# A list scheduler's model of TensorE: new durations, new latencies and a price for changing the shape of the product

## The chip, the cores and the metric

The kernel runs on one core of a Trainium2 chip. The metric is the device time of one execution in microseconds (us), taken as the median of several runs. Beside the runs there is one profiled execution, from which the trace comes; it has a time of its own.

A core has engines that work side by side, each through its own list of instructions and in the order of that list: PE (TensorE, matrix products and transposes), DVE (VectorE), ACT (ScalarE), POOL (GpSimd) and SP (SyncE, which here only sends DMA transfers). They wait for one another by semaphores.

## The reference

A trunk of two layers on x of shape (1, 256, 1024), all in float32. Each layer:

```python
h = rms_norm(x, attn_norm[l])
proj = h @ w_in[l]
r_q, r_k, r_v, r_g, n_q, n_kv, n_g, gm_z = jnp.split(proj, split_points, axis=-1)
ret_o = retention(rope(r_q), rope(r_k), r_v, r_g)          # 6 heads, chunks of 128
nsa_o = nsa(n_q, n_kv, n_g, ...)                           # 6 heads: compressed | selected | window, gated
gm_o  = spatial_gating(gm_z, gm_ws[l], gm_b[l])            # 4 heads of a causal gMLP
x = x + concatenate([ret_o, nsa_o, gm_o]) @ w_out[l]
h = rms_norm(x, ffn_norm[l])
gate, up = jnp.split(h @ w_gate_up[l], 2, axis=-1)         # d_ff = 2816
x = x + (silu(gate) * up) @ w_down[l]
```

Within `nsa`, queries and keys are normalised head by head, blocks of 32 keys and values are compressed to one token each by a small MLP (`cmp_w1`, gelu, `cmp_w2`), and three softmax outputs are mixed by sigmoid gates.

## The kernel before

Everything lies in SBUF for both row tiles of 128 positions; only the weights stream from memory. Each weight piece arrives in one of three buffers `wst`; ACT casts it to a rounded format (`whi`, fp32r, a "cast" below), DVE subtracts to get the rest (`wlo`, a "split" below), and PE multiplies in three terms: activations high with `whi`, high with `wlo`, low with `whi`. These products, 512 columns wide in most places (384 and 274 in some), are called main products here. They write to the four accumulators `acc`; all else of PE (transposes, scores, small products) goes through four banks `sm`. The activations are `hcat`, with a high and a low half.

A layer projects in seven parts: `nk` (keys), `nq` (queries), `gm` (gMLP), `nv` (values of the compression and the gates), `rq`, `rk`, `rg` (retention), each with 48 main products. What follows from a part runs beside the main products of the next ones. The steps that are spoken of below:

- `nk_tile` (keys): ACT squares, DVE sums (`nkr_ss`), ACT and DVE take the inverse root (`nkr_z`, `nkr_y`), DVE scales to `w1k`, PE transposes (`sm<-cst,w1k`), ACT and DVE write `Kh` and `Kl`. `nq_tile` does the same for the queries by `nqr_*`, `w2k` and `Q`, with three transposes for each row tile.
- `compress`: transposed tokens are copied by DVE to `aT`, PE multiplies them with `w` in 64 small products, and a gelu by single steps on DVE follows.
- `unit`: scores `sm<-Kh,Q` on PE, bias and row maximum on DVE (the custom instruction that writes `S`, a "mask step" below, printed as ISA in an order), exp on ACT, scaling by `asm` on DVE, transposes. `pv` multiplies with the values; its first product is `sm<-pcT,vbd`.
- `setup_bias`: POOL sends a small table to memory (`scr`) and reads it back as the bias `B`.

The order of the instructions isn't written by hand. The code of each step is a generator ("thread") that hands over operations; the class `Desk` (from L257) plays through the kernel with a model of time while it is built, and gives each engine its list in the order in which the model starts the operations. The model has a duration for each operation (`_cost_PE` from L199, and one for each other engine), a latency from an operation's end to its reader (`LAT`), and a price for a change of ACT's table. In `run` the engine that can start first is taken, and of its ready operations the one with the least `rank`: priority of the thread, then the time at which it became ready. A main product has the priority 1000, so any step that is ready goes before it; main products fill the rest. The model decides the order alone: on the chip every operation takes what it takes, and PE waits wherever its list names a product whose data isn't there.

All operations are issued by the one line L196, so the rows of the trace are told apart by the names of their tiles.

Of the kernel before, what the change touches and what calls it, by code (L numbers as in the profile page):

```python
# [166 lines left out]
class Op:  # L167
    def __init__(self, engine, call, dur, table, lat, prio, banks):
        self.engine, self.call, self.dur, self.table = engine, call, dur, table
        self.lat, self.prio, self.banks = lat, prio, banks  # L170


def _free(ap):
    n = 1
    for s in ap.shape[1:]:
        n *= s
    return n


def _psum(*aps):  # L180
    return any(getattr(a, "space", None) == bass.MemoryType.PSUM for a in aps)


class Engine:


# [3 lines left out]
    def __getattr__(self, method):  # L190
        fn = getattr(self.eng, method)

        def make(*a, prio=None, lat=True, **k):
            dur, table = getattr(self, "_cost_" + self.name)(method, a, k)
            banks = {x.tensor.name for x in (*a, *k.values()) if _psum(x)}
            return Op(self.name, lambda: fn(*a, **k), dur, table, lat, prio, banks)  # L196

        return make

    def _cost_PE(self, method, a, k):  # L200
        if method == "transpose":
            return 108, None
        n = _free(a[0])
        load = 0.42 * _free(a[1])
        if a[2].dtype == F32R:
            return max(0.422 * n, load + 27), None
        if a[0].shape[0] == 64 and a[0].base_partition() == 64:
            return 54 if n > 64 else 27, None
        return 2 * max(0.844 * n, 2 * load), None

    def _cost_DVE(self, method, a, k):
# [45 lines left out]


class Desk:
    LAT = {"PE": 170, "DVE": 150, "ACT": 190, "POOL": 200, "DMA": 2000, "SWDMA": 4500}  # L260
    TABLE = 1300
    COLD = 5500.0

    def __init__(self, preload):
        self.preload = preload
        self.free = {e: 0.0 for e in self.LAT}
        self.free["DMA"] = 1500.0
        self.pending = {e: [] for e in self.LAT}
        self.table = None
        self.cur = None  # L270
        self.live = 0
        self.after = 0
        self.banks = {}
        self.given = 100
# [74 lines left out]
    def run(self, gen):  # L349
        th = Thread(gen, 1000, 0.0)  # L350
        self.live = 1
        self._step(th, None)
        while self.live:
            best = None
            for e, reqs in self.pending.items():
                if reqs:
                    s = max(self.free[e], min(self._ready(r) for r in reqs))
                    if best is None or s < best[0]:
                        best = (s, e)
            assert best is not None, "every thread waits"  # L360
            now, e = best
            reqs = self.pending[e]

            def rank(r):
                th, ops = r
                p = ops[0].prio
                p = th.prio if p is None else p() if callable(p) else p
                if ops[0].table is not None and ops[0].table != self.table and now - th.t < 4000:
                    p += 500
                return (p, th.t, th.n)  # L370

            r = min((r for r in reqs if self._ready(r) <= now), key=rank)
            reqs.remove(r)
            th, ops = r
            t = now
            for op in ops:
                if op.table is not None and op.table != self.table:
                    t += self.TABLE
                    self.table = op.table
                    self.preload(op.table)  # L380
                op.call()
                t += op.dur * (2 if e == "PE" and t < self.COLD else 1)
            self.free[e] = t
            for op in ops:
                for b in op.banks:
                    self.banks.setdefault(b, {})[e] = t + self.LAT[e]
            th.t = t + (self.LAT[e] if ops[-1].lat else 0)
            self._step(th, None)


class Trunk:
# [71 lines left out]
    def stream_load(self):  # L463
        for i in range(L * len(PIECES)):
# [8 lines left out]
            self.st[i] = st  # L473
            self.desk.fire(self.loaded[i], self.desk.LAT["DMA"])
            if i < len(self.ev_w):
# [70 lines left out]
    def warm_up(self):  # L546
# [5 lines left out]
        while not self.started:  # L552
            n = 256 if self.desk.free["PE"] < Desk.COLD else 128
            yield self.PE.matmul(ps[:, :n], w[:, :128], w[:, :n], start=True, stop=True, lat=False, prio=2000)
# [3 lines left out]
    def load_start(self):  # L558

        SP, fire, lat = self.SP, self.desk.fire, self.desk.LAT["DMA"]  # L560
        yield SP.dma_start(self.ident, self.d["cst"][:, C_ID : C_ID + 128], lat=False)
# [1054 lines left out]
```

## Time and profile before

| | us |
|---|---|
| median of 3 runs | 646.93 (646.89 to 647.25) |
| profiled execution, its own time | 646.46 |
| span of the trace in it | 644.7 |
| mean granted clock of TensorE, share of full | 0.997 |
| PE busy | 635.1 |
| DVE busy | 452.9 |
| ACT busy | 364.8 |

A row of the timeline gives the start in us, the time that it takes, engine, line, operation, what it writes and reads, shapes, and with xN how many neighbouring instructions of that kind it holds together; in square brackets stands how long the engine was idle before it, and what released it. Ends of PE's products are modelled and overlap the next one, so the pace is read from starts.

### The profile page before, as it was taken

Reading aid. Unit: us, or ns where it says so; the run is one execution under the profiler, and the core shown is the slowest. Engines: PE = TensorE matmul, PEld = TensorE weight load, DVE = VectorE, ACT = ScalarE, POOL = GpSimd, SP = SyncE. Lnnn points to the kernel's source line nnn. Section 1 sums busy time; section 2 is a strip of 40 time slices with the busy share of each in tenths; the row PEclk is TensorE's granted clock in tenths of the full one; section 3 lists DMA queues with packets and bytes.
Section 4 is the critical chain, followed back from the end, with each engine's and each line's share of the span. In section 5 each row is a group of like instructions: output and inputs, shape, how many; then the busy total and the mean of one; then the engine's idle time right before and its main releaser. Section 6 shows DMA issues by size and latency. Waiting matters only on the chain.

```text
span 644.7 us, 9955 instructions
## 1 busy us (share of the span) xinstructions
PE 635.1 (99%) x3628; PEld 533.6 (83%) x3628; DVE 452.9 (70%) x1046; ACT 364.8 (57%) x685; POOL 11.0 (2%) x28
## 2 busy tenths in 40 slices
PE   8979999999999999999999999999999999999998
PEld 7768887788888888888887888788888888888886
DVE  5867988488677677664388899865867677776441
ACT  7648963576456555543377795444755555545330
POOL 0120000000000000010000000000000000000000
PEclk9999999999999999999999999999999999999999
DMA  8885245157555565566546522534665556565631
GB/s 257 284 228 175 91 123 181 66 166 231 190 180 192 185 196 192 185 257 204 163 135 196 196 92 64 173 110 149 186 191 185 193 195 187 174 197 184 192 114 65
DMA packets 32816, 111.63 MB, mean 173 GB/s; under 512 B 4339, under 2 KB 4851, under 8 KB 32512
## 3 DMA queue, kind: packets, MB, share of 16 engines
q1 hardware_dynamic: 32256, 109.86, 52.4%
q0 software_dynamic: 512, 1.14, 0.9%
q8 instruction: 28, 0.46, 0.3%
q14 instruction: 20, 0.16, 0.1%
HBM read 109.64 MB, written 1.35 MB: 172 GB/s over the span
## 4 chain that ended last, share of the span: by engine, by line
PE 89%; DMA 5%; ACT 2%; DVE 2%; issue 1%; SPq 0%; ACTq 0%
PE acc L196 60%; PE sm L196 29%; DMA wst<-in_wts_dram 5%; ACT whi L196 1%; DVE wlo L196 1%; DMA x<-in_x_dram 1%; DVE x L196 0%; SPq L196 0%; ACT w2k L196 0%; ACT L402 0%; ACT L196 0%; DVE Kl L196 0%; ACT Kh L196 0%; ACT hcat L196 0%; ACT w1k L196 0%
## 5 line engine op out<-in xcount | busy, mean ns | idle before, releaser
L196 DVE TENSOR_TENSOR wlo<-wst,whi 128x1024 fp32r<-128x1024 f32 (+3 forms) x204 | 245.0, 1202 | 140.8 <-ACT whi L196 139.6
L196 ACT CAST whi<-wst 128x1024 fp32r<-128x1024 f32 (+3 forms) x204 | 209.2, 1028 | 195.0 <-issue 49.7
L196 PE MATMUL acc<-whi,hcat 128*128 128x512 f32 (+2 forms) x512 | 141.2, 381 | 0.0
L196 PEld LDWEIGHTS acc<-whi,hcat 128*128 128x128 f32 x512 | 91.6, 189 | 15.0 <-issue 0.7
L196 PE MATMUL acc<-hcat,whi 128*128 128x512 f32 x320 | 101.2, 396 | 0.0
L196 PE MATMUL sm<-hcat,whi 128*128 128x512 f32 x320 | 99.7, 392 | 0.0
L196 PE MATMUL acc<-wlo,hcat 128*128 128x512 f32 (+2 forms) x256 | 80.6, 381 | 0.0
L196 PEld LDWEIGHTS sm<-hcat,whi 128*128 128x128 f32 x320 | 60.0, 188 | 14.2
L196 PEld LDWEIGHTS acc<-hcat,wlo 128*128 128x128 f32 x320 | 58.8, 188 | 11.7
L196 PE MATMUL sm<-hcat,wlo 128*128 128x256 f32 x320 | 64.4, 282 | 0.0
L196 PE MATMUL acc<-hcat,wlo 128*128 128x256 f32 x320 | 64.1, 282 | 0.0
L196 PEld LDWEIGHTS acc<-wlo,hcat 128*128 128x128 f32 x256 | 46.8, 189 | 7.8 <-issue 0.3
L196 PEld LDWEIGHTS acc<-hcat,whi 128*128 128x128 f32 x320 | 50.9, 190 | 1.7
L196 PE MATMUL acc<-whi,ah 128*128 128x512 f32 (+1 forms) x176 | 50.0, 378 | 0.0
L196 PE MATMUL acc<-whi,al 128*128 128x512 f32 (+1 forms) x176 | 50.0, 378 | 0.0
L196 PE MATMUL acc<-wlo,ah 128*128 128x512 f32 (+1 forms) x176 | 49.9, 377 | 0.0
L196 PEld LDWEIGHTS sm<-hcat,wlo 128*128 128x128 f32 x320 | 49.6, 190 | 0.0
L196 PEld LDWEIGHTS acc<-whi,ah 128*128 128x128 f32 x176 | 31.9, 188 | 5.5
L196 PEld LDWEIGHTS acc<-wlo,ah 128*128 128x128 f32 x176 | 31.8, 188 | 5.5
L196 PEld LDWEIGHTS acc<-whi,al 128*128 128x128 f32 x176 | 31.8, 188 | 5.5
L196 ACT ACTIVATE hcat<-sm,par 128x128 fp32r<-128x128 f32 x64 | 18.6, 379 | 9.2 <-PE sm L196 9.2
L196 DVE SCALAR_TENSOR_TENSOR hcat<-sm,par,hcat 128x128 fp32r<-128x128 f32 x64 | 18.5, 344 | 4.5 <-ACT hcat L196 4.5
(212 smaller groups left out, 726.6 us busy)
## 6 DMA issues: line engine op xcount, KB each, us to landing
wst<-in_wts_dram SPq DMA_DIRECT2D x186, 512.0 KB, 3.8
wst<-in_wts_dram SPq DMA_DIRECT2D x8, 384.0 KB, 3.0
w<-in_w_dram SPq DMA_DIRECT2D x2, 1024.0 KB, 7.0
wst<-in_wts_dram SPq DMA_DIRECT2D x4, 411.0 KB, 4.4
x<-in_x_dram SPq DMA_DIRECT2D x4, 256.0 KB, 5.3
wst<-in_wts_dram SPq DMA_DIRECT2D x4, 256.0 KB, 3.3
cst<-in_cst_dram SPq DMA_DIRECT2D x1, 768.0 KB, 5.3
B<-scr POOLq DMA_DIRECT2D x4, 192.0 KB, 6.2
```

Source lines behind the costliest of these rows:

```text
L196: return Op(self.name, lambda: fn(*a, **k), dur, table, lat, prio, banks)
```

## The change

The arithmetic is untouched. The model of `Desk` gets other numbers and one more rule:

- a main product costs max(0.417 n + 13, 2 load + 5) ns and not max(0.422 n, load + 27); at 512 columns that is 226.5 for 216;
- a half-array product (one with 64 partitions in its output or its stationary operand, the new `_tiled`) costs 27 where its base is partition 64, whatever its width, also by the second operand's base;
- the latency to readers is 216 for PE (170 before), 140 for DVE (150), 160 for ACT (190);
- PE is charged 100 (`LOAD`) when it has been idle, and 95 or 130 (`SWITCH`) when the kind of product changes, to half-array or back;
- among PE's ready operations of the same priority, those of the kind that ran last go first.

```diff
+def _tiled(a):
+    return a[0].shape[0] == 64 or a[1].shape[0] == 64
...
+            op = Op(self.name, lambda: fn(*a, **k), dur, table, lat, prio, banks)
+            op.tiled = self.name == "PE" and _tiled(a)
+            return op
...
         if a[2].dtype == F32R:
-            return max(0.422 * n, load + 27), None
-        if a[0].shape[0] == 64 and a[0].base_partition() == 64:
-            return 54 if n > 64 else 27, None
+            return max(0.417 * n + 13, 2 * load + 5), None
+        if _tiled(a) and 64 in (a[0].base_partition(), a[1].base_partition()):
+            return 27, None
...
 class Desk:
-    LAT = {"PE": 170, "DVE": 150, "ACT": 190, "POOL": 200, "DMA": 2000, "SWDMA": 4500}
+    LAT = {"PE": 216, "DVE": 140, "ACT": 160, "POOL": 200, "DMA": 2000, "SWDMA": 4500}
     TABLE = 1300
+    LOAD = 100
+    SWITCH = (130, 95)
...
-                return (p, th.t, th.n)
+                return (p, e == "PE" and ops[0].tiled != self.tiled, th.t, th.n)
...
             t = now
+            if e == "PE" and now > self.free[e]:
+                t += self.LOAD
             for op in ops:
...
+                if e == "PE" and op.tiled != self.tiled:
+                    t += self.SWITCH[op.tiled]
+                    self.tiled = op.tiled
```

The lists of SP and POOL come out the same. Those of PE, DVE and ACT change in many places. Three of them follow, with the order of before first and that of after behind it.

PE in layer 0, while the products of `gm` run: the transposes of the queries (`sm<-cst,w2k`).

```order
L196 MATMUL acc_63<-whi_76,hcat 128x512
L196 MATMUL acc_64<-whi_76,hcat 128x512
L196 MATMUL sm_68<-cst,w2k_91 128x128 x3
L196 MATMUL sm_70<-cst,w2k_88 128x128 x3
L196 MATMUL acc_63<-whi_76,hcat 128x512
L196 MATMUL acc_64<-whi_76,hcat 128x512
L196 MATMUL acc_63<-wlo_82,hcat 128x512
L196 MATMUL acc_64<-wlo_82,hcat 128x512
L196 MATMUL acc_63<-whi_76,hcat 128x512
L196 MATMUL acc_64<-whi_76,hcat 128x512
L196 MATMUL acc_65<-whi_77,hcat 128x274
```

```order
L201 MATMUL acc_64<-whi_76,hcat 128x512
L201 MATMUL sm_70<-cst,w2k_91 128x128 x3
L201 MATMUL sm_67<-cst,w2k_88 128x128 x3
L201 MATMUL acc_63<-whi_76,hcat 128x512
L201 MATMUL acc_64<-wlo_82,hcat 128x512
L201 MATMUL acc_63<-wlo_82,hcat 128x512
L201 MATMUL acc_64<-whi_76,hcat 128x512
L201 MATMUL acc_63<-whi_76,hcat 128x512
L201 MATMUL acc_64<-whi_76,hcat 128x512
L201 MATMUL acc_63<-whi_76,hcat 128x512
```

Six main products of `gm` were left behind the transposes before; now there are eleven, so the transposes stand five main products earlier (behind the 133rd of the kernel, where they stood behind the 138th).

DVE in layer 0, around the copies to `aT` that the compression's products read; ISA rows without a tile `S` read a maximum out, `wlo` rows are splits.

```order
L196 TENSOR_TENSOR wlo_83<-wst_74,whi_77 128x1024
L196 TENSOR_SCALAR gx<-gx 128x36
L196 COPY aT_130<-sm_68 64x2x64
L196 RECIPROCAL gate<-gx 128x36
L196 COPY aT_130<-sm_70 64x2x64
L196 COPY aT_130<-sm_68 64x2x64
L196 COPY aT_130<-sm_70 64x2x64
L196 RECIPROCAL asm_648<-asm_648 128x2
L196 ISA S_0_144,amx_675<-sm_69,B 128x128
```

```order
L201 ISA S_0_144,amx_688<-sm_69,B 128x128
L201 ISA amx_688 128x1
L201 RECIPROCAL asm_663<-asm_663 128x2
L201 TENSOR_SCALAR gx<-gx 128x36
L201 TENSOR_TENSOR wlo_83<-wst_74,whi_77 128x1024
L201 RECIPROCAL gate<-gx 128x36
L201 TENSOR_TENSOR gmr_z<-gmr_z,gmr_ss 128x4 x2
L201 TENSOR_TENSOR asm_663<-asm_663,gate 128x2
L201 SCALAR_TENSOR_TENSOR gmr_y<-gmr_z,gmr_y 128x4
L201 COPY aT_130<-sm_70 64x2x64
L201 TENSOR_SCALAR S_0_145<-S_0_145,asm_663 128x256
L201 COPY aT_130<-sm_67 64x2x64
```

The copies stood ahead of the mask steps of `S_0_144`; now all four of those, a reciprocal and steps of the gMLP norm and the gate stand ahead of the copies. Two more copies follow the last row.

DVE in layer 1, the inverse root of the keys (`nkr_*`) and their scaling to `w1k`.

```order
L196 SCALAR_TENSOR_TENSOR nkr_z<-nkr_y 128x2 x2
L196 TENSOR_TENSOR nkr_z<-nkr_z,nkr_ss 128x2 x2
L196 SCALAR_TENSOR_TENSOR nkr_y<-nkr_z,nkr_y 128x2
L196 COPY aT_2923<-sm_70 64x2x64
L196 SCALAR_TENSOR_TENSOR nkr_y<-nkr_z,nkr_y 128x2
L196 TENSOR_TENSOR w1k_97<-acc_63,nkr_y 128x256
L196 TENSOR_TENSOR w1k_94<-acc_64,nkr_y 128x256
```

```order
L201 TENSOR_TENSOR wlo_87<-wst_75,whi_81 128x1024
L201 SCALAR_TENSOR_TENSOR nkr_z<-nkr_y 128x2 x2
L201 TENSOR_TENSOR wlo_82<-wst_73,whi_76 128x1024
L201 TENSOR_TENSOR nkr_z<-nkr_z,nkr_ss 128x2 x2
L201 SCALAR_TENSOR_TENSOR nkr_y<-nkr_z,nkr_y 128x2 x2
L201 TENSOR_TENSOR wlo_83<-wst_74,whi_77 128x822
L201 TENSOR_TENSOR w1k_96<-acc_64,nkr_y 128x256
L201 TENSOR_TENSOR w1k_94<-acc_63,nkr_y 128x256
```

Three splits now stand within the chain or just ahead of it; before it ran through with one copy in it. On PE the transposes that read `w1k` stand 13 main products later than before (behind the 1479th).

## Rows read from the trace of the kernel before

**Rows 1.** The page's busy table: us, share of the span, instructions.

```profile
PE 635.1 (99%) x3628; PEld 533.6 (83%) x3628; DVE 452.9 (70%) x1046; ACT 364.8 (57%) x685; POOL 11.0 (2%) x28
```

**Rows 2.** Waits of PE: total us, times, longest us.

```profile
PE sm L196 <- DVE w2k L196: 4.9, 2, 3.5
...
PE sm L196 <- DVE Kl L196: 0.2, 1, 0.2
```

**Rows 3.** Timeline of PE (start, us, instruction), a stretch of main products only.

```profile
340.87 1.07 PE L196 MATMUL acc<-whi,hcat 128*128 128x512 f32 x4
341.77 0.39 PE L196 MATMUL acc<-wlo,hcat 128*128 128x512 f32 x1
```

**Rows 4.** Timeline from 33 to 48, what the query transposes waited for.

```profile
33.09 0.74 POOL L196 DMA_DIRECT2D scr<-w2k  x1 [12.64 <-ACT w2k L196]
...
35.38 0.33 SPq L196 DMA_DIRECT2D wst<-in_wts_dram  x1
...
43.80 2.27 POOL L196 DMA_DIRECT2D B<-scr  x4 [9.97 <-DMA scr<-w2k]
44.55 1.43 ACT L196 CAST whi<-wst 128x822 fp32r<-128x822 f32 x2 [6.10 <-DMA wst<-in_wts_dram]
45.46 1.02 DVE L196 TENSOR_TENSOR wlo<-wst,whi 128x822 fp32r<-128x822 f32 x1 [5.70 <-ACT whi L196]
...
47.20 1.54 PE L196 MATMUL sm<-cst,w2k 128*128 128x128 f32 x6 [3.48 <-DVE w2k L196]
```

**Rows 5.** Busy time by window; behind the engines the granted clock, DMA share, GB/s.

```profile
48.00:52.00 4.00, 4.00 (x20) 3.52 (x19) 3.69 (x6) 3.13 (x5) 0.00 (x0) 0.68 1.02 220
```

**Rows 6.** Timeline from 58 to 66, the way to the compression in layer 0.

```profile
57.99 0.50 PE L196 MATMUL sm<-Kh,Q 128*128 128x512 f32 x1 [0.24 <-DVE Kl L196]
...
58.45 1.06 ACT L196 CAST whi<-wst 128x1024 fp32r<-128x1024 f32 x1
...
59.09 0.37 DVE L196 TENSOR_SCALAR gx<-acc,negr 128x18 f32<-128x18 f32 x2
...
60.06 1.22 DVE L196 TENSOR_TENSOR wlo<-wst,whi 128x1024 fp32r<-128x1024 f32 x1
...
61.20 0.28 DVE L196 CUSTOM_DVE_ANT_0 S<-sm,B 128x128 f32<-128x128 f32 x1
...
62.88 1.22 DVE L196 TENSOR_TENSOR wlo<-wst,whi 128x1024 fp32r<-128x1024 f32 x1
...
64.59 0.74 DVE L196 COPY aT<-sm 64x128 f32<-64x128 f32 x3
...
65.36 0.17 DVE L196 RECIPROCAL asm<-asm 128x2 f32<-128x2 f32 x1
...
65.82 0.90 PE L196 MATMUL sm<-aT,w 128*64 128x33 f32 x22
```

**Rows 7.** Timeline at 348, the keys of layer 1.

```profile
347.71 0.62 PE L196 MATMUL acc<-wlo,hcat 128*128 128x512 f32 x2
...
348.01 0.74 DVE L196 TENSOR_TENSOR w1k<-acc,nkr_y 128x256 f32<-128x256 f32 x2
348.47 0.77 PE L196 MATMUL sm<-cst,w1k 128*128 128x128 f32 x4
```

**Rows 8.** Timeline of PE from 113, main products and half-array products in turn.

```profile
113.04 0.62 PE L196 MATMUL acc<-whi,hcat 128*128 128x384 f32 x2
113.59 0.57 PE L196 MATMUL sm<-rv,S 128*64 128x64 f32 x12
...
115.64 0.44 PE L196 MATMUL acc<-whi,hcat 128*128 128x384 f32 x1
115.92 0.51 PE L196 MATMUL acc<-wlo,hcat 128*128 128x384 f32 x2
```

**Rows 9.** Timeline at 98, the attention's output products in layer 0.

```profile
98.14 0.37 ACT L196 COPY pcT<-sm 96x256 f32<-96x256 f32 x1 [1.31 <-PE sm L196]
...
98.64 0.62 PE L196 MATMUL sm<-pcT,vbd 96*128 96x256 f32 x2
```

More of the change, by code (lines that the diff above doesn't have):

```diff
@@ L195, in make @@
             banks = {x.tensor.name for x in (*a, *k.values()) if _psum(x)}
-            return Op(self.name, lambda: fn(*a, **k), dur, table, lat, prio, banks)
+            op = Op(self.name, lambda: fn(*a, **k), dur, table, lat, prio, banks)
+            op.tiled = self.name == "PE" and _tiled(a)
+            return op
         return make
@@ L269, in __init__ @@
         self.table = None
+        self.tiled = False
         self.cur = None
```

## The prediction

> **What bounds the kernel now.** I read the busy table first: PE works 99% of the span, 635.1 of 644.7 us, no other engine more than 70% [rows 1]. Next the waits of PE: beside some start-up waits there are 4.9 us on `w2k`, the longest 3.5, and 0.2 on `Kl` [rows 2]. So a change that leaves the work alone can take away about 6 us at most, while any new wait of PE is paid in full. Third, the pace of the stream: in the main products (128x512, fp32r) four take from 340.87 to 341.77, that is 0.90/4 = 0.226 us each [rows 3]. The old table put 0.216 there and the new one puts 0.2265; I use 0.226 to turn places into time.
>
> The largest wait stands at 47.20, where the six transposes of the queries (`sm<-cst,w2k`) sat 3.48 us. Reading upward in the same view: DVE, which writes `w2k`, began the 822-wide split at 45.46 and came to the query steps only behind it. That split had waited 5.70 us for ACT's cast, and the cast 6.10 us for a weight transfer, sent at 35.38. The `scr` write, sent at 33.09, was in flight until POOL could go on at 43.80 [rows 4]. So a late transfer is the root. An engine here works through its list in order, and the small query steps are behind the split on DVE. [...]
>
> **The change, part by part.** No instruction of arithmetic is added or removed. The lists of SP and POOL, which issue every DMA, keep their order word for word; PE, DVE and ACT change theirs. So the cost is which consumer now comes earlier or later than its producer. I went through the places at which PE has least slack.
>
> *The switch term.* Grouping lowers the changes between whole-array and half-array products on PE from 56 to 48, that is four detours fewer. A detour of before: two 384-wide products ahead of it take 113.04 to 113.59, 0.55 where two at 0.17 each (0.226 x 384/512) take 0.35, so 0.20 to enter; behind it one takes 115.64 to 115.92, 0.28 for 0.17, so 0.11 to leave [rows 8]. Four times 0.31 is 1.2. The detours that were merged are of both lengths and some stand beside waits, so I take two thirds: -0.8, between -0.4 and -1.4.
> The upper end is worked out from another row: the last 512-wide product of a stretch has a record of 0.39, while the next one could begin after 0.226; if each change has to let that difference of 0.17 run out, eight give 1.4 [rows 3]. [...]
>
> *The query wait.* The transposes now stand behind the 133rd main product, not the 138th. DVE's list is the same there, with the split still ahead of the query steps, and the late transfer is issued in the same order. PE arrives 5 x 0.226 = 1.13 us earlier and waits 1.13 us longer; the products that it has not done come afterwards, with no loss of work. So the time in front of the next tight place is +1.13 late at most, less 0.24 that PE now waits for `Kl` at 57.99 [rows 6], about +0.9. It is not added by itself, because the next place decides both.
>
> *The compress stage of layer 0.* In before the four `aT` copies end on DVE at 64.59 + 0.74 = 65.33, and PE starts the products on `aT` at 65.82 with no wait; they follow main product 215 in both orders [rows 6]. In after, the copies move back on DVE's list: ahead of them stand four more mask steps (12, not 8; eight took 61.20 to 62.88, 0.21 each, so 0.84), and six short steps (a reciprocal, three of the gMLP norm, one of the gate, one scaling of `S`; the record of the reciprocal is 0.17 long and overlaps its neighbours, so I take 0.14 each, 0.84 in all, an estimate). The chain also starts behind the first split, which now leads it: its cast ends at 58.45 + 1.06 = 59.5, and before the same chain began at 59.09, so +0.41. Together 0.41 + 0.84 + 0.84 = 2.1, and the copies end at 67.4. PE would read at 65.82, so it waits 1.6 us. If PE also arrives 0.9 late from the query wait, it waits 0.7 here, and the sum of both is again 1.6. **+1.6**, from 0.5 (DVE finds the mask steps' inputs earlier, and the small steps overlap) to 2.5 (both delays add, because DVE too is late).
>
> *The keys of layer 1.* In before the key chain runs through on DVE, with `w1k` written from 348.01 and the transposes at 348.47, where PE, whose two products from 347.71 were done by 348.16, had 0.31 to wait [rows 7]. In after three splits of weights are mixed into the chain, 1.14 + 1.14 + 0.92 = 3.2 us by their spacing (a 1024-wide one took 60.06 to 61.20 [rows 6], an 822-wide one is 822/1024 of that); PE reaches the transposes 13 main products later, 13 x 0.226 = 2.9. The first of the two `w1k` products, which released the transposes at about 348.4, would be done at 348.4 + 3.2 = 351.6, with the casts that the splits need up to 0.5 later, PE at 348.16 + 2.9 = 351.1. The new wait is 0.5 to 1.0 where 0.31 was; I take **+0.7**, from 0.2 to 1.5.
>
> *All else.* Four more places have a slack under 0.5 us in the new order by the same counting (in layer 0 the first score product, in layer 1 the `aT` products, one update of `x`, one `rstd`). A wait of the size of the `Kl` one, 0.24, at one or two of them is **+0.3**, from 0 to 1.0.
>
> Sum: 1.6 + 0.7 - 0.8 + 0.3 = +1.8. The profiled execution took 646.46 us, so 648.3; it lies 0.47 below the median of the runs shown, 646.93, so **648.7** to compare with that.
>
> **The rivals.**
> *N, the waits stay covered, only the switches count.* DVE is busy 70%, and a model with better durations could place its steps so that the two moved chains arrive in time; then the sum is -0.8 + 0 to 0.8. For it: at 65.82 PE had no wait before, which shows that the old model got that right with worse numbers. Against: the hand count above. Time 646.1 to 646.9.
> *R, faster: the drain at full price and covered waits.* -1.4 and no new wait: 645.5. Or, on the same side, the query wait goes: it needs the weight transfer to land before the `scr` write is in its way. SP sent the one at 35.38 and POOL the other at 33.09, 2.3 us apart [rows 4]; since neither list changes, PE's and ACT's shifts would have to move `scr` by as much, and I find no such shift. [...]
> *S, worse: the output products of the attention come too early.* In before ACT's copy of `pcT` starts at 98.14, just released by PE after 1.31 of waiting, and PE takes it up at 98.64 [rows 9]. In after these products stand at main product 286, not 310, 24 x 0.17 = 4 us earlier in 384-wide products, and their softmax chain on DVE does not get shorter. If that chain, with the delay of the compress stage in front of it, is over 2 us late, PE stops: +2 to +4 on top, 650.7 to 652.7. Against: the scores themselves are earlier too.
> *Z, it does not act.* Excluded: three of the five lists differ.
>
> **How the numbers follow.** Forecast 0.45 (its own range 647.2 to 650.5), N 0.20, R 0.20 (drain 0.13, query wait 0.07), S 0.15. A measurement here can tell about 0.2% from no change, that is 645.6 and 648.2. N gives "same", R "faster", S "slower"; of the forecast's own range the lower quarter, 0.12, falls within 0.2%. Faster 0.20, same 0.32, slower 0.48. The range must hold 8 in 10: I leave out the vanished query wait (0.07) and the upper half of S (0.08), and go from 645.0 (drain at 1.4 less half of one more detour) to 651.7.
>
> **What would show it.** In the waits of PE: `w2k` near 4.6 at its longest instead of 3.5; a new wait on `aT` near 66 of 0.5 to 1.6; `w1k` near 351 of 0.5 to 1.0; the sum of all about 8 to 9 us, where it was 6.2. PE's busy time should fall by about 0.8, by rows such as 0.55 for two 384-wide products becoming fewer. I am wrong in mechanism if the `w2k` wait falls, if `aT` shows no wait, or if PE's busy time moves by more than 1.5. I am wrong in size if the transfer issued at 35.38 lands at another time, which the orders cannot tell.

## The result

The changed kernel takes **650.47 us** in the median of 6 runs (649.01 to 652.37), the kernel before 646.85 (646.70 to 647.25): a ratio of 1.0059, 95% interval 1.0047 to 1.0072. On another chip it was 651.01 against 646.28, 1.0066 (1.0051 to 1.0081). So it is slower, by 3.6 to 4.7 us, where +1.8 was forecast. The executions of after also differ among themselves, by 3.4 us on the first chip and 2.2 on the second; the first trace below is from the slowest one (652.37 us, span 650.6), a second one, called after_again, from one of 651.16.

The busy table of after, which answers to [rows 1]:

```profile
PE 636.5 (98%) x3626; PEld 534.1 (82%) x3626; DVE 451.4 (69%) x1046; ACT 369.5 (57%) x687; POOL 10.6 (2%) x28
```

The span grew by 5.9 us: PE is busy 1.4 us longer and idle 4.5 us longer. The plan of after has one start-up product of PE less (two rows) and two table loads of ACT more, 1.28 us each; the other instructions are the same ones in another order. The waits of PE in after, for [rows 2] (total us, times, longest us):

```profile
PE sm L201 <- DVE w2k L201: 5.6, 2, 4.2
PE sm L201 <- DVE w1k L201: 2.2, 2, 1.9
PE sm L201 <- DVE rstd L201: 1.0, 1, 1.0
PE acc L201 <- ACT whi L201: 0.6, 1, 0.6
PE sm L201 <- DVE x L201: 0.4, 1, 0.4
PE sm L201 <- DVE hx L201: 0.4, 1, 0.4
PE acc L201 <- DVE nr_i L201: 0.3, 1, 0.3
```

They add up to 10.5 us; in before it was 6.2. No single wait carries the loss. To see where it arises, here are the times at which the N-th main product starts (and the fourth row of the products on `aT`, and the last end on PE), from the traces laid against the orders. The count is that of the prediction, and the points are such that PE has done the same products before them in all three traces, but for the one start-up product:

| us | before | after | after_again |
|---|---|---|---|
| 124th main product | 40.15 | 41.11 | 40.94 |
| products on `aT`, layer 0 | 65.91 | 68.02 | 68.12 |
| 483rd | 154.81 | 156.72 | 156.71 |
| 1423rd | 337.69 | 340.19 | 340.04 |
| 1557th | 367.89 | 372.12 | 371.12 |
| 2138th | 515.72 | 521.65 | 520.43 |
| end | 641.53 | 647.45 | 646.23 |

Read by differences, after_again loses 0.8 up to the 124th product, 1.4 more up to `aT`, regains 0.3 up to the 483rd, and loses 0.4, 0.9 and 1.5 in the next three stretches: 4.7 in all. The first trace differs from it mainly between the 1423rd and the 1557th, the keys of layer 1: 1.7 instead of 0.9.

**The query wait**, timeline of after, for [rows 4]:

```profile
42.70 0.84 PE L201 MATMUL acc<-whi,hcat 128*128 128x512 f32 x3
...
43.63 2.27 POOL L201 DMA_DIRECT2D B<-scr  x4 [10.06 <-DMA scr<-w2k]
43.79 0.88 ACT L201 CAST whi<-wst 128x822 fp32r<-128x822 f32 x1 [5.30 <-DMA wst<-in_wts_dram]
...
44.70 1.02 DVE L201 TENSOR_TENSOR wlo<-wst,whi 128x822 fp32r<-128x822 f32 x1 [5.42 <-ACT whi L201]
...
45.06 0.88 ACT L201 CAST whi<-wst 128x822 fp32r<-128x822 f32 x1 [0.39 <-DMA wst<-in_wts_dram]
...
45.97 1.02 DVE L201 TENSOR_TENSOR wlo<-wst,whi 128x822 fp32r<-128x822 f32 x1
...
47.70 1.54 PE L201 MATMUL sm<-cst,w2k 128*128 128x128 f32 x6 [4.17 <-DVE w2k L201]
```

In before one 822-wide piece was late and its split stood before the queries. Here two are: the first one has landed only at 43.76 as well (its cast at 43.79 waited 5.30 us; the row of before with that cast follows), so both splits, 1.02 each, come in front of `w2k`. The second one sets the wait: it starts at 45.97, right behind its cast, which began when its transfer had landed, at 45.03. PE arrived at about 43.5 and waited 4.17 us. The first 822-wide cast in the timeline of before, with no wait:

```profile
37.37 0.87 ACT L196 CAST whi<-wst 128x822 fp32r<-128x822 f32 x1
```

That the first piece adds nothing to the wait shows in the run hold_keys (experiment 5), whose lists are the same up to here. There the first piece came early, the second was late as in before, and the longest wait for `w2k` is 4.2 us all the same:

```profile
38.38 0.88 ACT L201 CAST whi<-wst 128x822 fp32r<-128x822 f32 x1 [0.33 <-DMA wst<-in_wts_dram]
...
45.60 1.02 DVE L201 TENSOR_TENSOR wlo<-wst,whi 128x822 fp32r<-128x822 f32 x1 [5.13 <-ACT whi L201]
```

```profile
PE sm L201 <- DVE w2k L201: 5.7, 2, 4.2
```

Behind the wait the clock is low for longer in this trace. Busy time by window, with the granted clock as the third number from the end, for [rows 5]; after:

```profile
48.00:52.00 4.00, 4.00 (x13) 3.35 (x12) 2.55 (x6) 1.34 (x3) 0.79 (x6) 0.50 1.01 324
```

The granted clock was 0.50 for the whole window, where before had 0.68. The full clock is back at 50.6 in before (0.95 from 50.5 to 51.0) and at 53.6 in after (0.88 from 53.5 to 54.0). In after_again it is back at 51.3, after 3.4 us at 0.50, as many as in before, so the order alone does not make that stretch longer; this is worked out from the means, 0.59 from 48 to 52 and 0.76 from 47 to 54, where before has 0.68 and 0.76.

**The compress stage**, timeline of after_again, for [rows 6]:

```profile
66.81 0.28 DVE L201 COPY aT<-sm 64x128 f32<-64x128 f32 x1
...
67.25 0.32 PE L201 MATMUL sm<-aT,w 128*64 128x33 f32 x2
67.27 0.79 DVE L201 COPY aT<-sm 64x128 f32<-64x128 f32 x3
...
68.12 2.11 PE L201 MATMUL sm<-aT,w 128*64 128x33 f32 x60 [0.56 <-DVE aT L201]
```

The copies end at 68.06, where the prediction had 67.4; PE gets there at 67.25 by itself, delayed by the query wait, and waits 0.56 more.

**The keys of layer 1**, timeline of after, for [rows 7]:

```profile
350.29 1.05 ACT L201 CAST whi<-wst 128x1024 fp32r<-128x1024 f32 x1 [1.47 <-DMA wst<-in_wts_dram]
...
351.25 0.29 ACT L201 ACTIVATE nkr_y<-nkr_z 128x2 f32<-128x2 f32 x2
351.38 1.23 DVE L201 TENSOR_TENSOR wlo<-wst,whi 128x1024 fp32r<-128x1024 f32 x1 [2.48 <-ACT whi L201]
...
354.14 1.02 DVE L201 TENSOR_TENSOR wlo<-wst,whi 128x822 fp32r<-128x822 f32 x1
355.18 0.76 DVE L201 TENSOR_TENSOR w1k<-acc,nkr_y 128x256 f32<-128x256 f32 x2
355.66 0.77 PE L201 MATMUL sm<-cst,w1k 128*128 128x128 f32 x4 [1.89 <-DVE w1k L201]
```

A cast that waits 1.47 us for its transfer stands between the two ACT steps of the key chain, and the splits behind it on DVE stand in the same chain. In after_again the same cast waits 0.82 and PE 1.05.

### The profile page after: what moved, and what is told of

It reads as the page before. It is cut to its first block, busy times and chain, and to the rows that moved or that the text cites. A ratio compares the mean times of both kernels' runs of the same rounds, so it can differ in the third digit from the quotient of the medians.

```text
span 650.6 us, 9987 instructions
## 1 busy us (share of the span) xinstructions
PE 636.5 (98%) x3626; PEld 534.1 (82%) x3626; DVE 451.4 (69%) x1046; ACT 369.5 (57%) x687; POOL 10.6 (2%) x28
## 4 chain that ended last, share of the span: by engine, by line
PE 76%; DMA 8%; DVE 8%; ACT 5%; issue 2%; SPq 0%; ACTq 0%; DVEq 0%
PE acc L201 49%; PE sm L201 27%; DMA wst<-in_wts_dram 8%; DVE wlo L201 4%; ACT whi L201 3%; DVE hcat L201 1%; DVE S L201 1%; ACT w2k L201 1%; DVE x L201 1%; ACT L201 1%; ACT hcat L201 0%; ACT L417 0%; SPq L201 0%; DVE ro L201 0%; ACT Q L201 0%
## 5 line engine op out<-in xcount | busy, mean ns | idle before, releaser
L201 PE MATMUL acc<-whi,hcat 128*128 128x512 f32 (+2 forms) x512 | 143.2, 384 | 0.6 <-ACT whi L201 0.6
L201 PE MATMUL acc<-wlo,hcat 128*128 128x512 f32 (+2 forms) x256 | 78.2, 380 | 0.3 <-DVE nr_i L201 0.3
L201 PE MATMUL sm<-hcat,wlo 128*128 128x256 f32 x320 | 64.5, 282 | 0.0
L201 ACT ACTIVATE S<-S,amx 128x256 f32<-128x256 f32 (+1 forms) x48 | 21.2, 450 | 0.0
```

Source lines behind the costliest of these rows:

```text
L201: op = Op(self.name, lambda: fn(*a, **k), dur, table, lat, prio, banks)
```

## The experiments

**1. The change again**, and **2, 3. one layer each.** For the halves the model of `Desk` gets its new or old numbers when a layer's layout begins:

```diff
         for l in range(L):
+            if l == 1:
+                Desk.model(...)    # l0_new: back to the old numbers; l1_new: the new ones from here
```

> The changed kernel once more, unaltered, for a second trace. Theory A (the cost is fixed by the new order: three chains on DVE now stand behind more weight splits, so their readers on TensorE wait in every execution): median 650 to 651, the trace again with a wait on w2k of 3.8 to 4.4 near 47, on w1k of 1.5 to 2.2 near 355 and on rstd of about 1 near 473. Rival B (the executions differ by 3 us because the waits hang on when weight transfers land, so the w1k wait of layer 1 was large by chance in the first trace): the w1k wait below 1.2 in a trace whose time is under 650.

> The new model is used while layer 0 is laid out, the old one from the start of layer 1 on. By the lag of the main products in the first trace of after, layer 0 cost 2.4 of the 5.9 us and layer 1 3.5. Theory A (the two layers add up): +2.0 to +2.8 on before, 649.2 near the middle, wait on w2k as in after, no large wait on w1k at 350. Rival B (layer 0's delay is given back or is what makes layer 1 late): +0.8 or less, or +3.5 or more.

> The old model for layer 0, the new one from the start of layer 1 on; the other half of the pair. Theory A: +1.2 to +3.4 on before, of which a wait on w1k near 350 makes 1 to 1.8 and one on rstd near 470 about 1; the two halves together equal the whole change within 1 us. Rival B: within 0.5 us of before, since layer 1's chains are only late when layer 0 is.

Measured: after_again 651.01, 1.0066; l0_new 648.63, 1.0036 (1.0024 to 1.0049); l1_new 648.12, 1.0031 (1.0018 to 1.0043), against 646.28. That is +2.35 and +1.84 by the medians; the halves' ratios add up to 1.0067. So each half of the change brings about half of the loss, and neither needs the other. The `w1k` wait is 1.05 in after_again: the extra 0.84 of the first trace was a late transfer, as rival B said, though the time stayed over 650. One thing doesn't fit the expectation that layer 1 is clean with the old numbers: l0_new has a `w1k` wait of 1.03 in layer 1 all the same. Its plan of layer 1 starts from another state, and the splits fall into the key chain there too. Its trace loses 0.8 us from the 1423rd to the 1557th product, so the equal halves are those of the two plans, and not of the time lost in each layer.

**4. Is it the clock?** Products of the identity with itself are put ahead of the query transposes in after, once, in layer 0 (the edit is shortened here):

```diff
+        if l == 0 and not hasattr(self, "filled"):
...
+                for _ in range(17):
+                    self.nc.tensor.matmul(pt[:, 384:], self.ident, self.ident, start=True, stop=True)
+                return first()    # the first of the transposes
```

> After, with 17 products of the identity with itself put on TensorE's list right ahead of the query transposes of layer 0, some 3.7 us into a free part of the bank, so that TensorE works while it would wait there. Order and all else as in after. Theory A (the long idle time of 4.2 us is followed by 5.7 us at the lower clock, which costs about 2.8 us): the granted clock stays 1.0 from 47 to 54 and the time falls by 2 to 3 us below after. Rival B (the lower clock costs little, the wait itself is the whole price): the time within 0.5 us of after, although the clock stays up. Rival C (the products last longer than the wait and push the transposes back): up to 1 us slower.

Measured 649.99 (649.46 to 652.42), 1.0066: rival B in the time. The median lies 1.0 below that of after_again on the same chip, the mean of the six executions, 650.5, is the same. Its window and PE rows with the waits (the 17 products have two rows each):

```profile
48.00:52.00 4.00, 4.00 (x25) 3.56 (x24) 1.74 (x3) 1.55 (x3) 1.52 (x10) 1.00 0.99 348
```

```profile
42.57 3.96 PE L808 MATMUL sm<-cst 128*128 128x128 f32 x34
46.90 1.01 PE L201 MATMUL sm<-cst,w2k 128*128 128x128 f32 x6 [0.38 <-DVE w2k L201]
...
57.57 0.50 PE L201 MATMUL sm<-Kh,Q 128*128 128x512 f32 x1 [0.38 <-DVE Kl L201]
...
64.07 0.95 PE L201 MATMUL sm<-cst,w1k 128*128 128x128 f32 x4 [0.70 <-ACT w1k L201]
...
67.22 2.21 PE L201 MATMUL sm<-aT,w 128*64 128x33 f32 x62 [0.56 <-DVE aT L201]
```

The clock stays at 1.00, and PE is up to 2.2 us ahead of after_again, at the 147th main product; 0.6 of that it had at the 124th, before the filled place. Then it waits for `Kl` (0.38), for `w1k` (0.70) and for `aT` (0.56), and reaches the fourth row on `aT` at 67.23 instead of 68.12. Beyond the earlier start 0.3 us is left. The low clock is real and costs the stage nearly nothing: DVE and ACT decide when the products on `aT` can start.

**5. Is it the splits in the key chain?** In after, the casts and splits of three pieces of layer 1 wait in the plan until both key tiles are scaled:

```diff
+            if i - len(PIECES) in (11, 12, 13):    # in stream_hi and in stream_lo
+                yield self.keyed
```

> After, with one delay in the plan: in layer 1 the casts and the splits of three weight pieces (the 12th to 14th of the layer) are not planned before both key tiles are scaled. DVE then runs the key chain through, and the three splits follow; some 30 rows of the three lists move, the rest stays. Theory A (these splits, and the casts that they wait for, make the keys late): the w1k wait near 354 falls from 1.0 to 1.9 down to 0.3 or less and the time falls by 0.7 to 1.0 below after, to about 650.0 (ratio to before 1.0045 to 1.0055 where after has 1.0059 to 1.0066). Rival B (the pieces are then late for their main products, so the wait only moves): no w1k wait, but one on wlo or whi within the next 20 us, time as after.

Its trace shows what theory A said; the key chain runs through and PE doesn't wait:

```profile
348.88 0.75 DVE L201 TENSOR_TENSOR w1k<-acc,nkr_y 128x256 f32<-128x256 f32 x2
...
349.37 0.76 PE L201 MATMUL sm<-cst,w1k 128*128 128x128 f32 x4
```

From the 1423rd to the 1557th main product it takes 29.9 us, where after_again takes 31.1 and before 30.2, and the later stretches last as in after_again. The profiled execution took 649.72. But the median is 650.44, 1.0065 (1.0051 to 1.0080), no less than after's. So the price of the splits, 1.1 us, shows in this trace and not in the timed runs, whose executions spread over 2.5 us. In the last batch hold_both was to settle it and could not. Its lists in this stage are those of hold_keys, and PE waited for `w1k` in spite of the delay:

```profile
345.55 1.05 ACT L201 CAST whi<-wst 128x1024 fp32r<-128x1024 f32 x1 [0.72 <-DMA wst<-in_wts_dram]
...
349.92 0.77 PE L201 MATMUL sm<-cst,w1k 128*128 128x128 f32 x4 [0.92 <-DVE w1k L201]
```

A cast ahead of the delayed ones had to wait for its transfer there, and ACT's part of the key chain stands behind it. So the wait for `w1k` hangs on the landing of transfers, and taking the three splits away removes it in one trace and not in the other.

**6 to 8. Which numbers of the model?** dur_only takes the new durations of PE alone; no_pack takes durations and latencies; pack_only takes `LOAD`, `SWITCH` and the rule on kinds with the old durations and latencies. The latencies alone were not tried.

> Of the new model only the durations of TensorE's products are used; latencies, the charges for idle and for a change of kind, and the rule on kinds are the old ones. In the list this gives 48 changes of kind, as after has, for 56 before, and the query transposes behind main product 132. Theory A (the loss is from the query transposes and the two DVE chains, which any order with earlier transposes has): +2 to +4.5 on before, with a w2k wait of 3.8 to 4.4. Rival B (latency and kind rule do the harm): within 1 us of before.

> Of the new model only the charges and the rule on kinds of product are used, with the old durations and latencies. 54 changes of kind for 56 before; query transposes behind main product 138, as before. Theory A: one detour fewer is worth 0.3, and no chain moves behind splits, so -0.5 to +0.7 on before, w2k wait 3.4 to 3.6. Rival B (the rule on kinds itself delays steps that are waited for): +1 or more, with a new wait on TensorE.

> The new durations and latencies, without the charges and the rule on kinds. 48 changes of kind in the list, query transposes behind main product 133. Theory A (durations and latencies move the chains): +2 to +4.5 on before, w2k wait 4.1 to 4.4. Rival B (it is the combination with the kind rule): within 1.5 us of before.

| | median, us | ratio | changes of kind | longest `w2k` wait | longest `w1k` wait |
|---|---|---|---|---|---|
| dur_only | 649.42 | 1.0051 (1.0036 to 1.0067) | 48 | 3.8 | 1.3 |
| no_pack | 650.40 | 1.0058 (1.0044 to 1.0071) | 48 | 3.8 | 0.9 |
| pack_only | 645.84 | 0.9992 (0.9983 to 1.0002) | 54 | 2.7 | 0.5 |

All three against 646.36. The durations alone bring most of the loss, and the fall of the changes of kind to 48 too; the rule that is meant for it gives 54 alone, and costs nothing. In the times theory A held in all three. In the `w2k` wait it missed twice: 3.8 in no_pack for 4.1 to 4.4, and 2.7 in pack_only for 3.4 to 3.6, where PE arrived later, from a start that was 1.3 us late.

**9 to 12. Take the query wait away.** In the plan the split of the second 822-wide piece waits for the inverse roots of the queries, so that the query steps stand ahead of it on DVE:

```diff
             yield self.split_hi[i]
+            if i == 14:
+                yield self.queried
             self.lo[i] = yield Need(self.wlo)
```

> Before, with one delay in the plan: in layer 0 the split of the 15th weight piece (the second 822-wide one, whose transfer is the late one) is not planned before the query tiles have their inverse roots; on DVE the query steps then stand ahead of that split. Theory A (the query wait is DVE's list: the steps are ready by 40, and stand behind a split that waits for the transfer): no wait on w2k near 45, granted clock 1.0 throughout, time down by 3 to 5 us on before, 642 to 644. Rival B (the chain to the products on aT decides the end of this stage, as the run with the filled wait showed for after): the w2k wait is gone, but waits on Kl, w1k or aT take its place, and the time falls by less than 1.5.

> The same delay for the same split, in after. Theory A: the w2k wait of 4.2 falls away with the low clock behind it, and the time falls by 3 to 6 us below after, to 645 to 647.5. Rival B (aT decides): by less than 1.5 us, with a larger wait on aT or w1k near 64.

> After with both delays, the one for the queries of layer 0 and the one for the keys of layer 1. By the traces of after and hold_keys the stage of layer 1's keys is 1.1 us shorter with the second delay, but the medians showed nothing. Theory A (it is worth 1 us, hidden by the spread of the executions): 0.7 to 1.3 below hold_q_after on the same chip, no w1k wait near 350. Rival B (given back later): within 0.4 of hold_q_after.

> The charges and the rule on kinds alone (the part of the change that gave 0.9992 of before), with the delay for the queries. Theory A: the two gains add, 0.3 to 0.7 below hold_q_before. Rival B (another order, other waits): 1 us or more above hold_q_before, with a wait on TensorE that the latter doesn't have.

Against 646.23: hold_q_before 646.10, 1.0000 (0.9989 to 1.0011); hold_q_after 649.92, 1.0044 (1.0026 to 1.0063), with two of its eleven executions at 645.3 and 645.9; hold_both 649.75, 1.0046 (1.0028 to 1.0064), 0.2 below hold_q_after, so rival B in the time; **hold_q_pack 641.77, 0.9941** (0.9923 to 0.9959), faster than both kernels. The largest wait of before is gone in hold_q_before, and nothing is gained; the start-up wait on `w2k` (1.4) is all that is left of it:

```profile
PE sm L196 <- DVE S L196: 2.2, 2, 1.9
PE sm L196 <- DVE w2k L196: 1.4, 1, 1.4
PE sm L196 <- DVE gx L196: 1.3, 1, 1.3
PE acc L196 <- DVE w1k L196: 1.0, 1, 1.0
PE sm L196 <- ACT w1k L196: 0.8, 1, 0.8
```

`S` (1.92, at 115.7), `gx` (1.28, at 59.3) and `w1k` (1.00, at 47.4) took its place. From the 124th to the 483rd product the waits add up to 4.5 us, where they were 3.8 in before, and the lower clock comes behind `S` instead, for 6.8 us (all windows from 42 to 70 have 1.00, the mean of the run is 0.995). That was rival B, though not at the tiles that it named. (The profiled execution took 647.67, the longest of the twelve. Its products on `aT` stand behind 14 more main products than in before, so their start tells nothing here.)

In hold_both the query wait is still there, 4.10:

```profile
44.88 1.02 DVE L201 TENSOR_TENSOR wlo<-wst,whi 128x822 fp32r<-128x822 f32 x1 [5.52 <-ACT whi L201]
...
46.83 1.54 PE L201 MATMUL sm<-cst,w2k 128*128 128x128 f32 x6 [4.10 <-DVE w2k L201]
```

The first 822-wide piece was late there, and its split, which is not delayed, stands in front of the query steps. In hold_q_after, whose lists are the same up to there, that piece came early and nothing waited. In these traces the delay takes the query wait away where the first piece is early, and not where it is late.

hold_q_pack has little of all this; these are all its waits:

```profile
PE sm L201 <- DVE w2k L201: 1.4, 1, 1.4
PE acc L201 <- DVE w1k L201: 0.7, 1, 0.7
PE sm L201 <- DMA x<-in_x_dram: 0.2, 1, 0.2
PE sm L201 <- ACT w1k L201: 0.2, 1, 0.2
```

It is neither of the expected sums: the gains don't add, each plan has waits of its own, and this one has few. From the 124th to the 483rd product it waits less than 1.0 us, where pack_only waits 4.4. Why this plan has so few was not tested.

hold_q_after's profiled execution (649.58) has no query wait. It waits 1.73 us for `aT`, reaches the fourth row there at 64.70, 3.4 ahead of after_again, and has given back 2.5 of it by the 483rd product: the products on `aT` and what follows run at the lower clock (0.50 in the windows from 65.0 to 71.5), 3.48 us for the products on `aT` that take 2.11 in after_again. What its executions at 645 have that the others lack no trace shows, since none of them was profiled.

## Why the prediction was right, and where not

- **What bounds the kernel.** Right: PE's work is unchanged, and what moved the time was waits of PE on chains whose steps an order puts behind weight splits.
- **The switch term**, -0.8. Right in sign, and too large. From `aT` to the 483rd product, with 29 changes of kind in before and 23 in after, PE's time less its waits is 88.9 us in before and 88.4 to 88.6 in the five traces with after's order there. From the 1557th to the 2138th, with 26 and 24, it is 147.6 in before and 147.6 to 147.8 in after, after_again, fill_after and hold_keys. So the term is worth 0.3 to 0.5 at most, by this comparison of traces, and the price read from one detour was too high. That every change lets the 0.17 of the last record run out, the drain in the range and in rival R, no run shows: six changes fewer in the first of these stretches go with the 0.3 to 0.5, two fewer in the second with no gain. The cause was named wrong too; the new durations did it, not the rule on kinds. And PE's busy time rose by 1.4, and by 1.1 in after_again, where it should have fallen. A part of that is the clock in the first trace, since products at the lower clock count as busy (from 48 to 52 PE is busy 4.00 of 4.00 us with 13 rows at 0.50 in after, and with 25 at 1.00 in fill_after): from the 124th product to `aT` PE's time less its waits is 22.7 there, 22.2 in after_again and 22.0 in before. The rest lies in the start and behind the 483rd product, as below.
- **The query wait.** Right that it gets longer: 4.17, where 4.6 was forecast, but in another way than counted. The transposes start 0.5 later than in before, since the second 822-wide transfer landed that much later, which the orders can't show. And PE came 0.2 earlier and not 1.13, because the start was 0.96 late. The clock's part was left out of the sum of after and turned out not to matter.
- **The compress stage**, +1.6. Right, in its reason too: `aT` is the next place and decides for both. Up to `aT` after_again loses 1.4 beyond what the start cost, and the filled wait showed that an earlier PE waits there. "If `aT` shows no wait, I am wrong" was too strong a test: the first trace has none, since PE came late enough.
- **The keys of layer 1**, +0.7. Right in size: 0.9 in after_again, 1.7 in the first trace with a later transfer. The reason is only in part shown: without the splits in the chain the wait was gone in hold_keys and 0.92 in hold_both, where a transfer was late.
- **All else**, +0.3, with at most 1.0. This is the step that failed. By the table above the total is 4.7; less 1.4 and 0.9, plus 0.3 for the stretch of the switches, 2.7 us are left for it. 0.8 of that is in the start, which the prediction didn't look at. Seven traces with this order of the start reach the 124th product 0.5 later on average than three with the old one, and they differ by 1.3 among themselves, so how much of it belongs to the order is open. 0.45 lies between the 483rd and the 513th product, beside the `rstd` and `w1k` transposes of layer 0, with no idle time over 0.1 us there; up to the 1423rd, six traces with after's order take 183.3 to 183.5 us for that stretch and five with the old one about 182.9. 0.35 is `hx`, and about 0.2 is spread. 0.9 is `rstd` at 473, which was named as tight and priced at a quarter of that. In after_again:

```profile
469.82 1.05 ACT L201 CAST whi<-wst 128x1024 fp32r<-128x1024 f32 x1 [2.51 <-DMA wst<-in_wts_dram]
...
470.90 1.23 DVE L201 TENSOR_TENSOR wlo<-wst,whi 128x1024 fp32r<-128x1024 f32 x1 [2.01 <-ACT whi L201]
...
472.63 0.49 PE L201 MATMUL sm<-cst,rstd 128*128 128x128 f32 x2 [0.92 <-DVE rstd L201]
```

  Here too a split that waits for a transfer stands ahead of the chain. Of the eight traces with after's order of that part four show the wait, 0.6 to 1.0, and in these the cast had waited 2.1 to 2.7 us for its transfer; in the other four it waited 1.4 at most, and PE did not wait.
- **The rivals.** S did not come: there is no wait on `pcT`. N was wrong, R too. The time, 650.47, lies in the forecast's own range at its upper end; the 651.01 of the other chip lies above that range. The gain from the switches was put too high by 0.3 to 0.5 and all else too low by 2.4, so that the time still fell into the range is due to its width, not to the sum.

## What to carry to other kernels

A model that is truer in its parts doesn't give a better list when the waits come from what it leaves out, here the landing of transfers: every order has its own places where a chain falls behind an unrelated long step, and only the sum over all of them counts. When a reordering is costed, count the many places with little slack as a term of their own, with a size taken from how many there are, not as a remainder. And removing the longest wait is worth only the distance to the next one: in before 3.5 us of waiting went and 0.0 of time, and with the charges and the rule on kinds alone 2.7 went and, by the ratios, about 3 of time.

## What the runs showed of the hardware

The first 822-wide transfer landed early in seven traces and late in seven. SP sends it close to the moment at which POOL sends the `scr` write (297 KB, 10.5 us to landing in after). From the issue and landing times in fourteen traces:

| issue of the transfer after that of `scr`, us | traces | its time to landing, us |
|---|---|---|
| -0.64 to +0.10 | before, l1_new, hold_q_before, hold_q_pack, pack_only | 4.7 to 5.0 |
| +0.33, +0.36 | hold_q_after, hold_keys | 4.3, 5.2 |
| +0.50, +0.52 | l0_new, after_again | 10.2, 10.4 |
| +0.74, +0.75 | no_pack, dur_only, fill_after, after, hold_both | 9.5 to 10.3 |

All that were sent 0.5 us or more behind the `scr` write landed within 0.6 us of its own landing; all that were sent up to 0.36 behind it landed 5.0 to 6.4 us before. This is a comparison of traces; no run moved the `scr` write alone. The rows show a step from 5 to 10 us between 0.36 and 0.50 us; what makes it was not shown.

The granted clock fell to 0.50 around the end of the query wait in before, after and seven other traces (in l0_new and after_again the windows, of 2 and 4 us, have means of 0.57 and 0.59), where PE had been idle for 3.5 to 4.3 us, and it stayed at 1.00 behind the one of 2.7 us in pack_only:

```profile
48.00:52.00 4.00, 4.00 (x29) 3.60 (x27) 3.90 (x8) 3.02 (x5) 0.00 (x0) 1.00 1.03 189
```

The length of the idle time isn't all of it: in hold_q_after the clock fell (0.90 from 64.5 to 65.0, 0.50 from there to 68.0) behind a wait of 1.7 us, shorter than the one in pack_only, and in hold_q_before behind the wait of 1.9 us for `S`. What else decides it was not shown. Holding the clock up saved no more than the 0.3 us up to `aT` in fill_after, and nothing in the time (ratio 1.0066, as in after_again).
